# A hybrid encoder layer on one core: re-stacking of rotated heads through DRAM, tokens normalised ahead, and side tasks emitted by a model of when shared PSUM banks are read

## The chip, the cores and the metric

One core of one Trainium2 chip runs the whole layer as one program. The metric is the device time of one execution in microseconds (us); lower is better. Engines are named as in the profile: PE (TensorE, matrix products), PEld (its weight loads), DVE (VectorE), ACT (ScalarE), POOL (GpSimd), and SP (SyncE), whose queue issues every DMA of this kernel.

## What is computed

One encoder layer over 2048 tokens of width 1024 in float32. The normalised tokens are projected to about 4.6 thousand columns. Three groups of heads use them: windowed attention (16 query heads, 4 key/value heads, rotary, a sink logit), a state-space group that is scanned in both directions in chunks of 128 tokens, and 4 heads of attention into 256 memory tokens. The three are concatenated to 2048 columns, multiplied by `w_out`, added to the input and normalised.

```python
hn = rms_norm(h, norm_in_w); proj = hn @ w_in
q = rotary(q); k = rotary(k)
att = window_attention(q, k, v, sink) * silu(g_attn)
y = ssd_scan(xs, dt_f, ...) + ssd_scan(reversed ...) + d_skip * xs
ssd = gated_group_rmsnorm(y, z, ssd_norm_w)
xat = softmax(qm @ mk) @ mv * silu(g_mem)
h = h + concat(att, ssd, xat) @ w_out
out = rms_norm(h, norm_out_w)
```

## The kernel before, in words

Every large product is made of three: each operand is split into a high part (a cast on ACT) and a low part (a subtraction on DVE, `split`, L170 to L173), and high*high, high*low and low*high are accumulated in one PSUM bank (`split3`, all recorded at L154).

**Main line.** Tokens are taken in four windows `c` = 3, 2, 1, 0 of about 512 tokens. For each window the kernel projects keys (`keys`, L346), values and step sizes (`values`, L361), then for four head groups `g` the queries and gates (`heads`, L463), the convolution inputs, the gate `z` and one memory head. `prep_x` (L317) loads the next window's raw tokens, multiplies them by the norm and splits them into the 16 tiles `xh` and `xl`. After the last window comes the output projection: `out_block(c)` (L979) for the 16 blocks of 128 tokens. Each makes 96 products: 48 on the attention rows 0 to 3 and the memory rows 12 to 15 of `mix_d`, then 48 on its rows 8 to 11 (state-space part) and 4 to 7. One block (15) does its first 48 earlier, in `early` (L963), while attention is finishing.

**Side tasks.** Attention blocks, memory attention, the local part of the scan (`ssd_local`, L581), the incoming states (`incoming`, L696) and the gated norm of the scan (`forward`, L725) are Python generators. PE's order is exactly the order in which the program emits its products; the other engines' order is chosen by the scheduler. Each product adds an assumed time to `clock`. Between pieces of the main line `tick` (L112) resumes every side task whose `yield` time has passed on that clock; `need(task)` (L131) lets the clock run, with nothing emitted by the main line, until a task is done. A task counts as done when its last instruction is emitted.

**The scan's end.** `forward(c)` starts when `forward(c-1)` is done, and the first when `ssd_local` of the last window is done. It loads `y_d` into `b0`, adds the incoming states, multiplies by `z`, squares, yields 15; a small product with `ones` sums the squares (`t<-ones`); yields 4; a second small product spreads the scale (`t<-yo`); DVE then scales `b0` in four instructions (L758) and SP stores it to rows 8 to 11 of `mix_d` (L760). `out_block(c)` calls `need(fwd[c])` before its second 48 products and loads these rows back as `mxl` (L947); ACT makes `mxh` of them, DVE the low part.

**PSUM.** `pj` has three banks for the main line; `s` and `t` have two and `o` one, shared by all side tasks. A product into a bank waits until the bank's last reader is done.

**Re-stacking.** `rope` (L207) rotates two projected tiles with four products on DVE and two sums on POOL. `heads` then copies 32-partition pieces into the tile `qs` with 16 small DMAs (L475), and `keys` stores 16 pieces to `k_d` (L358). `values` has one buffer `gm` for what it stores to `v_d` (L375), one DMA for each block.

Of the kernel before, what the change touches and what calls it, by code (L numbers as in the profile page):

```python
# [17 lines left out]
P = 128  # L18
# [27 lines left out]
def layer(ctx: ExitStack, tc: tile.TileContext, a: dict):  # L46
# [22 lines left out]
    k_d = dram.tile([2, NG, 64, L], F32, name="k_d")  # L69
# [13 lines left out]

    def bank(pl, name):
        return pl.tile([P, 512], F32, name=name)

# [120 lines left out]
    def rope(pa, pb, cs, sn):  # L207
        n = cs.shape[-1]
        t1, t2, t3 = (misc.tile([P, CH], F32, name=f"rt{i}")[:, :n] for i in range(3))
        nc.vector.tensor_tensor(t1, pa, cs, ALU.mult)  # L210
        nc.vector.tensor_tensor(t3, pa, sn, ALU.mult)
        nc.vector.tensor_tensor(t2, pb, sn, ALU.mult)
        nc.gpsimd.tensor_tensor(t1, t1, t2, ALU.subtract)  # L213
        nc.vector.tensor_tensor(t2, pb, cs, ALU.mult)
        nc.gpsimd.tensor_tensor(t3, t3, t2, ALU.add)
        res = []
        for i, t in enumerate((t1, t3)):
            hi = as32r(misc.tile([P, CH], F32, name=f"r{'ht'[i]}{i}")[:, :n])
            split(hi, as32r(t), t)
            res.append((hi, as32r(t)))  # L220
        return res
# [95 lines left out]
    def prep_x(c, rb, raw=None):  # L317
        s, _ = window(c)
        w = CH * (c + 1) - s
        hs, ls = [], []  # L320
        for kt in range(KT):
            if raw is None:
                x32 = (misc.tile([P, XW + 6], F32, name="raw", bufs=2) if kt == 3 else
                       misc.tile([P, XW], F32, name="th", bufs=2) if kt in (4, 5) else
                       misc.tile([P, XW], F32, name="cu", bufs=3))[:, :w]
                nc.sync.dma_start(x32, a["xT"][kt * P:(kt + 1) * P, s:s + w])
                src = x32
            else:
                src = raw[kt]
                x32 = misc.tile([P, XW], F32, name="cu", bufs=3)  # L330
            nc.vector.scalar_tensor_tensor(x32, src, nw[:, kt:kt + 1], rb[:, :w], ALU.mult, ALU.mult)
            xh = xhl.tile([P, XW], F32R, name="xh")
            xl = xhl.tile([P, XW], F32R, name="xl")
            split(xh[:, :w], xl[:, :w], x32)
            hs.append(xh)
            ls.append(xl)
        return hs, ls

    def tables(t0, n):
        tab = misc.tile([P, 2, CH], F32, name="tab")[:, :, :n]  # L340
        nc.sync.dma_start(tab, a["trig"][:, :, t0:t0 + n])
        return tab[:, 0], tab[:, 1]
# [3 lines left out]
    def keys(c, xs):  # L346
# [4 lines left out]
        for o, pa in zip(range(0, e - s, n), pas):  # L351
            tab = tables(s + o, n)
            pb = yield from proj(wb, xs, o, n)
            res = rope(pa, pb, *tab)
            for j in range(2):
                for w in range(2):
                    for g in range(NG):
                        nc.sync.dma_start(k_d[w, g, j * 32:(j + 1) * 32, s + o:s + o + n],  # L358
                                          as32(res[j][w])[g * 32:(g + 1) * 32])

    def values(c, xs):  # L361
# [6 lines left out]
        for b in range(nb):  # L368
# [4 lines left out]
            v = misc.tile([P, CH], F32, name="gm")[:, :256]  # L373
            nc.scalar.mul(v, ps[:, :256], 0.5)
            nc.sync.dma_start(v_d[s // P + b], v)  # L375
# [3 lines left out]
    def steps(s, nb, raw):  # L379
# [21 lines left out]
        yield 8.0  # L401
# [6 lines left out]
        mm(pf[:, 256:256 + n], ones, raw.rearrange("p b r -> p (b r)"), True, True)  # L408
        fl = fc.rearrange("p b d r -> p (b d r)")
# [6 lines left out]
        yield 1.5  # L416
        pt = bank(ps_t, "t")
        nc.tensor.transpose(pt[:n, :P], fl, ident)
# [44 lines left out]
    def heads(c, xs, g, tab):  # L463
# [5 lines left out]
        res = rope(pa, pb, *tab)  # L469
        qs = ap_.tile([P, 4, CH], F32R, name="qs", bufs=2)  # L470
        for w in range(2):
            for j in range(2):
                for r in range(4):
                    o = w * 64 + j * 32
                    nc.sync.dma_start(as32(qs)[o:o + 32, r, :], as32(res[j][w])[r * 32:(r + 1) * 32])  # L475
# [7 lines left out]
    def attention(c, g, i, qs, gt, kv):  # L483
# [7 lines left out]
        if i == 4 * c:  # L491
            yield from take("kst", 1)
            kst = [ap_.tile([P, 6 * P], F32R, name=nm, bufs=2) for nm in ("khh", "kll")]
            for j in range(2):
                for u in range(2):
                    nc.sync.dma_start(as32(kst[j])[u * 64:(u + 1) * 64, :(hi + 1 - lo) * P],
                                      k_d[j, g, :, lo * P:(hi + 1) * P])
# [12 lines left out]
        for r in range(4):  # L510
            ss = bank(ps_s, "s")
            mm(ss[:, :w], qs[:, r, tl], kst[0][:, ks], True, False)
            mm(ss[:, :w], qs[:, r, tl], kst[1][:, ks], False, True)
            nc.vector.tensor_tensor_reduce(pm[:, r, :w], ss[:, :w], band[:, ms], 1.0,  # L514
                                           sink8[:, 4 * g + r:4 * g + r + 1], ALU.add, ALU.max, mx[:, r:r + 1])
            if r < 3:
                yield 1.2
# [13 lines left out]
        for n_, j in enumerate(order):  # L531
            if n_ == 2:
                yield 0.7
            tt = bank(ps_t, "t")
            for r in range(4):
                tr(tt[:, r * P:(r + 1) * P], pm[:, r, j * P:(j + 1) * P])
            if n_ == 1:
# [4 lines left out]
        held["pm"] += 4  # L542
        oo = bank(ps_o, "o")
        for j in order:
            vv = vg[:, k0 + j - lo]
            mm(oo[0:64, 0:256], vv, pts[j][:, 0:256], j == order[0], j == order[-1])
            mm(oo[64:128, 0:256], vv, pts[j][:, 256:512], j == order[0], j == order[-1])
        held["pt"] += nk
# [32 lines left out]
    def ssd_local(blocks):  # L581
# [3 lines left out]
        yield 5.0  # L585
        for i, (c, g) in enumerate(parts):
# [4 lines left out]
            xc, ee = nxt  # L591
            tt = bank(ps_t, "t")
            for j in range(3):
                tr(tt[:, j * P:(j + 1) * P], xc[:, j])
            nat = sp.tile([P, 3 * P], F32, name="nat", bufs=1)
            nc.scalar.copy(nat, tt[:, :3 * P])
            pc = bank(ps_s, "s")
            mm(pc[:, :P], xc[:, 2], xc[:, 3], True, True)
            cbm = sp.tile([P, 2, P], F32, name="cbm")
# [14 lines left out]
            yield 14.0  # L614
            py = bank(ps_o, "o")
            for pr in range(2):
                for u in range(2):
                    r = 2 * pr + u
                    mm(py[u * 64:(u + 1) * 64, pr * P:(pr + 1) * P], nat[:, r * 64:(r + 1) * 64], gg[:, r], True, True)
            yo = sp.tile([P, 2, P], F32, name="yo")  # L620
# [3 lines left out]
            nc.sync.dma_start(y_d[2 * g:2 * g + 2, :, c * P:(c + 1) * P].rearrange("j p t -> p j t"), yo)  # L624
            pst = bank(ps_s, "s")
            mm(pst, nat[:, 256:384], xd.rearrange("p d r e -> p (d r e)"), True, True)
            so = sp.tile([P, 2, 256], F32, name="carry")
# [22 lines left out]
    def mem_attention(c, hd, qh, ql, gm, mkt):  # L650
        yield 11.0
        pms = []
        for half in range(2):
            ss = bank(ps_s, "s")
            for j in range(2):
                tl = slice((2 * half + j) * P, (2 * half + j + 1) * P)
                for _ in split3(ss[:, j * MEM:(j + 1) * MEM], [(qh[:, tl], ql[:, tl], mkt[:, :MEM], mkt[:, MEM:])]):
                    pass
            mx = misc.tile([P, 2], F32, name="mmx", bufs=3)
# [16 lines left out]
        pts = []  # L676
        for m in range(2):
            tt = bank(ps_t, "t")
            for q in range(4):
                tr(tt[:, q * P:(q + 1) * P], pms[q // 2][:, q % 2, m * P:(m + 1) * P])  # L680
            hi = ap_.tile([P, 512], F32R, name="pt", bufs=3)
# [6 lines left out]
        yield 2.0  # L688
        oo = bank(ps_o, "o")
        for _ in split3(oo, [(mvt[:, 0, m], mvt[:, 1, m], pts[m][1], pts[m][2]) for m in range(2)]):  # L690
            pass
        held["pt"] += 2
# [3 lines left out]
    def incoming(c):  # L696
# [13 lines left out]
        yield 5.0  # L710
        for d, st_ in enumerate((state["f"], hbt)):
            py = bank(ps_s, "s")
            for pr in range(4):
                mm(py[:, pr * P:(pr + 1) * P], st_[:, pr * P:(pr + 1) * P], cc[:, pr // 2], True, True)
            nc.vector.tensor_tensor(ef[:, d], py.rearrange("p (q t) -> p q t", q=4), ef[:, d], ALU.mult)
            if d == 0:
                yield 1.0
# [7 lines left out]
    def forward(c):  # L725
# [18 lines left out]
        yield 15.0  # L744
        pn = bank(ps_t, "t")
        for g in range(2):
            mm(pn[:, g:g + 1], zv[:, g, 0], ones[:, 0:1], True, True)
# [343 lines left out]
```

## Time and profile before

| what | value |
|---|---|
| median of 3 runs | 1913.85 us (1912.57 to 1914.81) |
| the profiled execution | 1912.68 us |
| its span, first to last instruction | 1911.0 us |
| PE busy | 1780.5 us, 93% of the span |
| mean granted clock of TensorE | 0.973 of full speed |
| DMA queue | 305 MB, 52.9% of 16 engines' span |

The span is one execution as the profiler recorded it; the 1.7 us between it and that execution's time lie before the first and after the last instruction. Idle time of an engine is put down to what ended it. PE's share is the one near the span; the next is DVE with 62%.

### The profile page before, as it was taken

The page shows a single profiled execution, that of the slowest core. Times are in us where ns is not written, and L with a number is a line of the kernel's source. Part 1 is how long each engine was busy: PE and PEld are TensorE (multiplying, and loading weights), DVE is VectorE, ACT ScalarE, POOL GpSimd, SP SyncE. Part 2 cuts the span into 40 slices and gives each one's busy share as a digit, 9 for nine tenths or more (in the row PEclk, how much of TensorE's full clock was granted, in tenths as well). Part 3 has the DMA queues.
Part 4 walks back from the last instruction along what each step waited for, and adds up shares of the span by engine and source line. Part 5 has one row for each costly group of instructions (what it writes and reads, how often), then busy time and mean ns, then how long its engine had stood idle before and what let it go on. Part 6 is the DMA issues. An engine that isn't in the chain of part 4 may idle for free.

```text
span 1911.0 us, 27061 instructions
## 1 busy us (share of the span) xinstructions
PE 1780.5 (93%) x9242; PEld 1440.4 (75%) x9242; DVE 1187.4 (62%) x2709; ACT 928.7 (49%) x2006; POOL 331.5 (17%) x295
## 2 busy tenths in 40 slices
PE   6879999978999997999999989999898899999998
PEld 5767888856778785776778768776676688887886
DVE  6456566686776568677566778866775744333332
ACT  5247556563756555556456565456555521111111
POOL 0100000022220001222000012211222233323210
PEclk9989999999999999999999989999899999999999
DMA  6555343458654344756443457645456665555531
GB/s 226 155 149 168 117 131 112 121 167 251 204 170 138 103 133 138 220 181 189 135 136 111 131 179 234 194 134 176 146 181 192 201 196 166 166 164 171 160 122 55
DMA packets 254554, 306.75 MB, mean 161 GB/s; under 512 B 32848, under 2 KB 174928, under 8 KB 254416
## 3 DMA queue, kind: packets, MB, share of 16 engines
q1 hardware_dynamic: 254416, 305.02, 52.9%
q8 instruction: 73, 1.20, 0.3%
q14 instruction: 65, 0.53, 0.1%
HBM read 224.46 MB, written 63.70 MB: 151 GB/s over the span
## 4 chain that ended last, share of the span: by engine, by line
PE 59%; DVE 13%; DMA 13%; ACT 6%; issue 5%; SPq 2%; POOL 1%; DVEq 0%; ACTq 0%; POOLq 0%
PE pj L154 44%; PE s L154 7%; PE o L154 4%; PE t L158 3%; DVE wl L173 2%; DMA ws<-in_w_in_dram 2%; ACT pm L522 2%; DMA cu<-in_x_dram 2%; ACT wh L172 1%; DVE b L605 1%; ACT pm L526 1%; DVE pm L514 1%; DMA mxl<-mix_d 1%; DMA v_d<-gm 1%; PE t L154 1%
## 5 line engine op out<-in xcount | busy, mean ns | idle before, releaser
L154 PE MATMUL pj<-xh,wh 128*128 128x512 f32 (+2 forms) x1296 | 508.8, 393 | 9.2 <-ACT xh L172 6.5
L154 PE MATMUL pj<-xl,wh 128*128 128x512 f32 (+2 forms) x1296 | 498.0, 384 | 11.3 <-DVE xl L173 11.2
L154 PE MATMUL pj<-xh,wl 128*128 128x512 f32 (+2 forms) x1296 | 496.3, 383 | 0.8 <-DVE wl L173 0.7
L173 DVE TENSOR_TENSOR wl<-ws,wh 128x1024 fp32r<-128x1024 f32 (+2 forms) x175 | 219.1, 1253 | 117.9 <-ACT wh L172 111.8
L154 PEld LDWEIGHTS pj<-xl,wh 128*128 128x128 f32 x1296 | 248.0, 191 | 50.9 <-DVE xl L173 16.6
L154 PEld LDWEIGHTS pj<-xh,wh 128*128 128x128 f32 x1296 | 248.3, 192 | 49.2 <-ACT xh L172 7.6
L154 PEld LDWEIGHTS pj<-xh,wl 128*128 128x128 f32 x1296 | 247.5, 191 | 46.2 <-DVE wl L173 1.6
L172 ACT CAST wh<-ws 128x1024 fp32r<-128x1024 f32 (+2 forms) x175 | 179.9, 1028 | 153.6 <-PE pj L154 103.5
L522 ACT ACTIVATE pm<-pm,mx 128x385 f32<-128x385 f32 (+1 forms) x256 | 151.4, 594 | 78.1 <-DVE mx L520 78.0
L514 DVE CUSTOM_DVE_ANT_0 pm<-s,band,sink 128x384 f32<-128x384 f32 (+1 forms) x256 | 149.5, 595 | 58.9 <-PE s L154 56.6
L154 PE MATMUL pj<-woh,mxh 128*128 128x512 f32 x416 | 169.1, 406 | 1.9 <-ACT woh L172 1.9
L154 PE MATMUL pj<-wol,mxh 128*128 128x512 f32 x416 | 164.6, 396 | 2.0 <-DVE wol L173 2.0
L154 PE MATMUL pj<-woh,mxl 128*128 128x512 f32 x416 | 164.4, 395 | 0.0
L526 ACT ACTIVATE pm<-pm,den 128x384 f32<-128x384 f32 (+1 forms) x256 | 133.1, 592 | 17.4 <-DVE den L524 17.4
L172 ACT CAST mxh<-mxl 128x512 fp32r<-128x512 f32 x64 | 39.3, 618 | 184.8 <-DMA mxl<-mix_d 99.4
L154 PE MATMUL s<-khh,qs 128*128 128x384 f32 (+1 forms) x256 | 96.3, 376 | 20.7 <-DMA qs<-rt 8.9
L158 PE MATMUL t<-ident,pm 128*128 128x128 f32 x736 | 105.6, 279 | 9.7 <-ACT pt L540 3.8
L540 ACT COPY pt<-t 128x512 f32<-128x512 f32 x120 | 69.9, 582 | 90.2 <-PE t L158 90.0
L158 PEld LDWEIGHTS t<-ident,pm 128*128 128x128 f32 x736 | 88.2, 143 | 31.4 <-issue 6.0
L213 POOL TENSOR_TENSOR rt<-rt,rt 128x512 f32<-128x512 f32 (+2 forms) x21 | 28.5, 1358 | 470.4 <-DVE den L524 202.6
L451 DVE SCALAR_TENSOR_TENSOR cu<-raw,cw,cu 128x512 f32<-128x512 f32 (+2 forms) x128 | 98.3, 775 | 15.0 <-ACT cu L449 14.4
L173 DVE TENSOR_TENSOR mxl<-mxl,mxh 128x512 fp32r<-128x512 f32 x64 | 48.7, 760 | 90.8 <-ACT mxh L172 90.8
(228 smaller groups left out, 3001.5 us busy)
## 6 DMA issues: line engine op xcount, KB each, us to landing
ws<-in_w_in_dram SPq DMA_DIRECT2D x152, 512.0 KB, 4.0
fb<-f_d SPq DMA_DIRECT2D x32, 512.0 KB, 4.9
mxl<-mix_d SPq DMA_DIRECT2D x64, 256.0 KB, 4.0
qs<-rt SPq DMA_DIRECT2D x192, 64.0 KB, 2.1
mix_d<-ao SPq DMA_DIRECT2D x64, 128.0 KB, 3.1
xc<-xbc_d SPq DMA_DIRECT2D x32, 256.0 KB, 4.0
st_d<-carry SPq DMA_DIRECT2D x32, 256.0 KB, 3.6
fb<-ef_d SPq DMA_DIRECT2D x32, 256.0 KB, 4.2
```

The lines of the kernel that those rows point to most:

```text
L154: nc.tensor.matmul(out, lhsT=lhsT, rhs=rhs, start=start, stop=stop)
L158: nc.tensor.transpose(out, in_, ident)
L172: nc.scalar.copy(hi, x)
L173: (eng or nc.vector).tensor_tensor(lo, x, as32(hi), ALU.subtract)
L213: nc.gpsimd.tensor_tensor(t1, t1, t2, ALU.subtract)
L451: nc.vector.scalar_tensor_tensor(u, raw[:, r0 + k:r0 + k + cnt], cw[:, i, k:k + 1], u, ALU.mult, ALU.add)
L514: nc.vector.tensor_tensor_reduce(pm[:, r, :w], ss[:, :w], band[:, ms], 1.0, sink8[:, 4 * g + r:4 * g + r + 1], ALU.add, ALU.max, mx[:, r:r ...
L522: nc.scalar.activation(pm[:, r, :w + 1], pm[:, r, :w + 1], AF.Exp, bias=mx[:, r:r + 1], scale=0.125, accum_out=den[:, r:r + 1])
L526: nc.scalar.activation(pm[:, r, :w], pm[:, r, :w], AF.Copy, scale=den[:, r:r + 1])
L540: nc.scalar.copy(pts[j], tt)
L605: nc.vector.tensor_scalar(gg[:, r], cbm[:, 0], dt[:, 0, hd], None, ALU.mult)
```

## The change

It makes five edits. (1) `rope` works on both halves in one tile with instructions of 1024 columns, all on DVE and ACT; `heads` stores the high and the low half to `q_d` in DRAM and loads each back in stacked form (4 DMAs for 16); `keys` stores 2 for 16; the table has three rows. (2) `norm_x`, called after `heads` of group 2, loads the next window's tokens, normalises them and stores them to `xn_d`; `prep_x` loads them from there and only splits. (3) `values` stores two blocks in one DMA from a tile with three buffers. (4) `bank` notes on `clock` until when each bank of `s`, `t` and `o` will be read; before each use a task yields until the bank is taken to be free (`slot`), and `reads` sets that time. Fixed yields change with it, among them 8 to 18 and 1.5 to 2 in `steps`, 5 to 12 in `ssd_local`, 5 to 7 in `incoming`, 4 to 5.5 in `forward`. (5) The first early block takes its weights one after the other for both halves of the columns.

```diff
+    turn = {"s": 0, "t": 0, "o": 0}
+    until = {"s": [0.0] * 2, "t": [0.0] * 2, "o": [0.0]}
     def bank(pl, name):
+        if name in turn:
+            until[name][turn[name] % len(until[name])] = clock[0] + 3.0
+            turn[name] += 1
         return pl.tile([P, 512], F32, name=name)
+    def slot(name, n=1):
+        while True:
+            u = until[name]
+            t = max(u[(turn[name] + i) % len(u)] for i in range(n))
+            if t <= clock[0]:
+                return
+            yield max(t - clock[0], 0.1)
+    def reads(name, us, back=1):
+        u = until[name]
+        u[(turn[name] - back) % len(u)] = clock[0] + us
...
+    def rope(pa, pb, tab):
+        n = tab.shape[-1]
+        t, u = (misc.tile([P, 2, CH], F32, name=f"rt{i}")[:, :, :n] for i in range(2))
+        nc.vector.tensor_tensor(t, pa.unsqueeze(1).broadcast_to([P, 2, n]), tab[:, 1:3], ALU.mult)
+        nc.vector.tensor_tensor(u, pb.unsqueeze(1).broadcast_to([P, 2, n]), tab[:, 0:2], ALU.mult)
+        nc.vector.tensor_tensor(t, t, u, ALU.add)
+        hi = as32r(misc.tile([P, 2, CH], F32, name="rt1")[:, :, :n])
+        split(hi, as32r(t), t)
+        return hi, as32r(t)
...
+    def norm_x(c, rb):
+        s, _ = window(c)
+        w = CH * (c + 1) - s
+        for kt in range(KT):
+            x32 = misc.tile([P, XW], F32, name="xp", bufs=4)[:, :w]
+            nc.sync.dma_start(x32, a["xT"][kt * P:(kt + 1) * P, s:s + w])
+            nc.vector.scalar_tensor_tensor(x32, x32, nw[:, kt:kt + 1], rb[:, :w], ALU.mult, ALU.mult)
+            nc.sync.dma_start(xn_d[kt, :, s:s + w], x32)
...
-        yield 8.0
+        yield 18.0
+        yield from slot("t")
         pf = bank(ps_t, "t")
...
-                    nc.sync.dma_start(as32(qs)[o:o + 32, r, :], as32(res[j][w])[r * 32:(r + 1) * 32])
+        for w, t in enumerate(rope(pa, pb, tab)):
+            nc.sync.dma_start(q_d[g % 2][w], as32(t))
+            nc.sync.dma_start(as32(qs)[w * 64:(w + 1) * 64], q_d[g % 2][w].rearrange("(r p) j t -> (p j) r t", r=4))
...
+            yield from slot("s")
             ss = bank(ps_s, "s")
             mm(ss[:, :w], qs[:, r, tl], kst[0][:, ks], True, False)
             mm(ss[:, :w], qs[:, r, tl], kst[1][:, ks], False, True)
+            reads("s", 1.7)
...
         nxt = ssd_load(*parts[0])
-        yield 5.0
+        yield 12.0
...
-        yield 4.0
+        yield 5.5
+        yield from slot("t")
         pn = bank(ps_t, "t")
         mm(pn[:, :2 * P], ones, dg.rearrange("p g t -> p (g t)"), True, True)
+        reads("t", 2.0)
```

How the order moves, at three places. First, PE in the output projection, at the fifth block (`c` = 4). `t<-yo` is the small product of `forward(4)`; `woh8` to `woh11` are the weights for rows 8 to 11 of `mix_d`; `mxh` and `mxl` with a number are the two halves of one loaded piece. Before, `forward(4)`'s product stands among the second products of block 2:

```order
L154 MATMUL pj_15389<-wol9_14960,mxh_15470 128x512
L154 MATMUL pj_15389<-woh9_14961,mxl_15468 128x512
L154 MATMUL t_15518<-yo_15490,ones_107 128x256
L154 MATMUL pj_15389<-woh10_14967,mxh_15470 128x512
L154 MATMUL pj_15389<-wol10_14966,mxh_15470 128x512
```

and 170 rows later, the products of block 4 on its rows 8 to 11 begin with `mxh_15845`:

```order
L154 MATMUL pj_15761<-wol15_14774,mxh_15769 128x512
L154 MATMUL pj_15761<-woh15_14775,mxl_15767 128x512
L154 MATMUL pj_15760<-woh8_14781,mxh_15845 128x512
L154 MATMUL pj_15760<-wol8_14780,mxh_15845 128x512
L154 MATMUL pj_15760<-woh8_14781,mxl_15843 128x512
```

In the changed kernel the same block reads, with no row between the two:

```order
L177 MATMUL pj_15327<-wol15_14334,mxh_15335 128x512
L177 MATMUL pj_15327<-woh15_14335,mxl_15333 128x512
L177 MATMUL t_15397<-yo_15364,ones_110 128x256
L177 MATMUL pj_15326<-woh8_14341,mxh_15414 128x512
L177 MATMUL pj_15326<-wol8_14340,mxh_15414 128x512
L177 MATMUL pj_15326<-woh8_14341,mxl_15412 128x512
```

All 16 blocks of the changed kernel read like this: 16 `t<-yo`, each followed directly by the first product on `woh8` of its own block. For blocks 0 and 15 `t<-ones` also stands directly before `t<-yo`.

Second, SP at the same block of the changed kernel: `b0_15221` is what `forward(4)` scaled, `mxl_15412` the piece that the products above need.

```order
L1037 DMA xr_15521<-in_x_dram 128x1024
L807 DMA mix_d_102<-b0_15221 128x4x128
L776 DMA b0_15404<-y_d_93 128x4x128
L993 DMA mxl_15412<-mix_d_102 128x4x128
L993 DMA mxl_15417<-mix_d_102 128x4x128
L993 DMA mxl_15511<-mix_d_102 128x4x128
```

Before, the store of `forward(4)` and the load of the same rows stand ten issues apart on SP; now only the next block's `y_d` load is between them.

Third, PE where attention ends and the scan's end begins. Before, the first products of `incoming` (`s<-cbm,state`) stand among the last attention blocks:

```order
L154 MATMUL s<-mkt,qh 128x256 x2
L154 MATMUL s<-mkt,ql 128x256
L154 MATMUL s<-cbm,state 128x128 x4
L154 MATMUL s<-khh,qs 128x384
L154 MATMUL s<-kll,qs 128x384
```

Now `ssd_local` is emitted up to row 5497 of PE's order, and they follow at row 5532, 84 rows later than before (row 5448), inside the early block's products:

```order
L181 MATMUL t<-ident,pm 128x128 x4
L177 MATMUL s<-cbm,state 128x128 x4
L177 MATMUL pj<-woh_14335,mxh 128x512
L177 MATMUL pj<-wol_14334,mxh 128x512
L177 MATMUL pj<-woh_14335,mxl 128x512
L177 MATMUL s<-cbm,b_14422 128x128 x4
```

In the first window, the step-size product `t<-dtraw` stands 42 projection products later than before (row 462 for row 420).

## Rows read from the trace of the kernel before

**Rows 1.** The page: busy time, share of the span and instructions of each engine.

```profile
PE 1780.5 (93%) x9242; PEld 1440.4 (75%) x9242; DVE 1187.4 (62%) x2709; ACT 928.7 (49%) x2006; POOL 331.5 (17%) x295
```

**Rows 2.** Stages: each engine's busy time and count, granted clock, DMA share, GB/s.

```profile
412.00:1462.00 1050.00, 990.74 (x5208) 785.97 (x5207) 736.04 (x1774) 601.51 (x1327) 174.87 (x153) 0.97 0.55 165
1462.00:1510.00 48.00, 32.29 (x177) 24.70 (x178) 35.61 (x76) 31.94 (x75) 20.24 (x14) 0.93 0.67 206
1510.00:1903.80 393.80, 391.17 (x1840) 320.64 (x1837) 154.22 (x307) 74.49 (x144) 100.53 (x93) 1.00 0.53 155
```

**Rows 3.** What PE waited for: us in total, times, longest.

```profile
PE pj L154 <- DVE xl L173: 11.2, 11, 1.6
PE t L154 <- DVE dtraw L400: 10.4, 1, 10.4
PE s L154 <- DVE mx L514: 9.3, 11, 2.1
...
PE s L154 <- DMA qs<-rt: 8.9, 3, 5.1
PE s L154 <- ACT mpm L665: 8.5, 6, 2.3
PE pj L154 <- ACT xh L172: 6.5, 2, 4.4
...
PE pj L154 <- ACT dtraw L376: 5.4, 2, 4.9
PE t L158 <- ACT pt L540: 4.0, 5, 1.4
...
PE o L154 <- DVE ao L550: 3.8, 3, 1.3
```

**Rows 4.** Three stretches, columns as in rows 2, each just after a wait of PE.

```profile
76.60:80.00 3.40, 3.39 (x15) 3.40 (x16) 1.40 (x4) 0.72 (x2) 2.00 (x2) 0.50 0.20 62
...
110.50:114.10 3.60, 3.60 (x12) 3.12 (x13) 1.09 (x3) 0.51 (x2) 1.04 (x1) 0.50 0.45 109
...
473.30:479.40 6.10, 6.10 (x17) 5.33 (x18) 3.48 (x10) 0.00 (x0) 0.00 (x0) 0.50 0.81 267
```

**Rows 5.** Chain of waits, 1684 to 1731: start, us, what.

```profile
1687.38 0.63 ACT mxh L172
...
1688.64 1.13 DVE b L758 x4
...
1689.78 2.27 DMA mix_d<-b
...
1707.65 0.08 DVE rn L749
...
1709.16 0.67 PE t L154 x2
```

**Rows 6.** DMA issues: line, queue, times, KB each, median us from issue to landing.

```profile
mxl<-mix_d SPq DMA_DIRECT2D x64, 256.0 KB, 4.0
...
mix_d<-b SPq DMA_DIRECT2D x16, 256.0 KB, 2.4
...
v_d<-gm SPq DMA_DIRECT2D x16, 128.0 KB, 4.7
```

**Rows 7.** Tile `mxl`, from 1530: min/median/max ns of each; us from issue to landing.

```profile
L173 DVE TENSOR_TENSOR mxl<-mxl,mxh x56: 677/692/1553, 1537.6 to 1879.2; 128x512 fp32r<-128x512 f32 x56
L947 SPq DMA_DIRECT2D mxl<-mix_d x55: 359/384/954, 1536.6 to 1870.4; - x55
...
DMA to landing us min/median/max: 2.5/4.0/5.7
```

**Rows 8.** Chain of waits, whole span: the last products after the last `t<-yo`.

```profile
1852.25 51.61 PE pj L154 x222
```

**Rows 9.** Tile `rt` (rotated heads): min/median/max ns of SP's copies to `qs`.

```profile
L475 SPq DMA_DIRECT2D qs<-rt x192: 507/588/1582, 108.8 to 1427.7; - x192
```

More of the change, by code (lines that the diff above doesn't have):

```diff
@@ L66, in layer @@
     misc = pool("misc", 1, stack=wx)
-    k_d = dram.tile([2, NG, 64, L], F32, name="k_d")
+    k_d = dram.tile([2, P, 2, L], F32, name="k_d")
+    q_d = [dram.tile([2, P, 2, CH], F32, name=f"q_d{i}") for i in range(2)]
+    xn_d = dram.tile([KT, P, L], F32, name="xn_d")
     xbc_d = dram.tile([8, P, L], F32, name="xbc_d")
@@ L339, in tables @@
     def tables(t0, n):
-        tab = misc.tile([P, 2, CH], F32, name="tab")[:, :, :n]
+        tab = misc.tile([P, 3, CH], F32, name="tab")[:, :, :n]
         nc.sync.dma_start(tab, a["trig"][:, :, t0:t0 + n])
-        return tab[:, 0], tab[:, 1]
+        return tab
     dts = {}
@@ L353, in keys @@
             pb = yield from proj(wb, xs, o, n)
[L354 to L359, printed above, removed]
+            for w, t in enumerate(rope(pa, pb, tab)):
+                nc.sync.dma_start(k_d[w, :, :, s + o:s + o + n], as32(t))
     def values(c, xs):
@@ L372, in values @@
                                  wv[k // 3][1][:, (k % 3) * NV:(k % 3 + 1) * NV]) for k in range(KT)])
-            v = misc.tile([P, CH], F32, name="gm")[:, :256]
-            nc.scalar.mul(v, ps[:, :256], 0.5)
-            nc.sync.dma_start(v_d[s // P + b], v)
+            if b % 2 == 0:
+                m = min(2, nb - b)
+                v = misc.tile([P, XW], F32, name="cu", bufs=3)[:, :m * 256].rearrange("p (m d) -> p m d", m=m)
+            nc.scalar.mul(v[:, b % 2], ps[:, :256], 0.5)
+            if b % 2 == m - 1:
+                nc.sync.dma_start(v_d[s // P + b - m + 1:s // P + b + 1].rearrange("b p d -> p b d"), v)
             nc.scalar.copy(raw[:, b, :], ps[:, 256:NV])
@@ L516, in attention @@
             if r < 3:
-                yield 1.2
+                yield 0.6
         if i == 4 * c + 3:
@@ L531, in attention @@
         for n_, j in enumerate(order):
-            if n_ == 2:
-                yield 0.7
+            yield from slot("t")
             tt = bank(ps_t, "t")
@@ L542, in attention @@
         held["pm"] += 4
+        yield from slot("o")
         oo = bank(ps_o, "o")
@@ L591, in ssd_local @@
             xc, ee = nxt
+            yield from slot("t")
             tt = bank(ps_t, "t")
@@ L614, in ssd_local @@
             yield 14.0
+            yield from slot("o")
             py = bank(ps_o, "o")
@@ L653, in mem_attention @@
         for half in range(2):
+            yield from slot("s")
             ss = bank(ps_s, "s")
@@ L676, in mem_attention @@
         pts = []
+        yield from slot("t", 2)
         for m in range(2):
@@ L687, in mem_attention @@
             pts[m] = tt, hi, lo
-        yield 2.0
+        yield 3.0
+        yield from slot("o")
         oo = bank(ps_o, "o")
@@ L691, in mem_attention @@
             pass
+        reads("o", 1.4)
         held["pt"] += 2
@@ L709, in incoming @@
             nc.sync.dma_start(ef[u * 64:(u + 1) * 64], ev[u].partition_broadcast(64))
-        yield 5.0
+        yield 7.0
         for d, st_ in enumerate((state["f"], hbt)):
+            yield from slot("s")
             py = bank(ps_s, "s")
@@ L744, in forward @@
         yield 15.0
+        yield from slot("t")
         pn = bank(ps_t, "t")
@@ L911, in layer @@
             with tc.high_priority(offset=200):
-                xs = prep_x(c - 1, rb)
-            idle(clock[0] + 0)
+                xs = prep_x(c - 1)
     need(mem_t)
@@ L968, in early @@
         nc.sync.dma_start(xr, a["x"][c * P:(c + 1) * P, :])
-        for n_ in products(pf, mh, ml, [(n_, k) for n_ in range(2) for k in mh], WO_K[0], WO_K[7]):
+        order = [(n_, k) for k in mh for n_ in range(2)]
+        if begun:
+            order.sort(key=lambda v: v[0])
+        for n_ in products(pf, mh, ml, order, WO_K[0], WO_K[7]):
             if n_ is not None:
```

63 lines of the change are left out of this document (27 added, 36 removed).

## The prediction

> **What bounds the kernel now.** I read the busy shares first: PE is busy for 1780.5 of 1911.0 us, the next engine, DVE, for 62% [rows 1]. So time is lost or won where PE stands still or runs at the lower clock. The stages say where that is: between 412 and 1462 PE lacks 59 of 1050 us, in the 48 us at the end of attention 16, but in the output projection from 1510 to 1903.8 only 2.6 of 393.8, at a clock of 1.00 [rows 2]. That stage has nothing to give and can only lose. The waits name the causes ahead of it, none over 11.2 us in total [rows 3]. A wait also costs clock: after waits of 4.9, 10.4 and 5.1 us [rows 3] PE was busy at a granted clock of 0.50, its lower level of 1.2 GHz, for 3.4, 3.6 and 6.1 us [rows 4].
>
> **The change, part by part.**
>
> *The scan's end against the output projection.* This decides. `forward` yields longer and starts later (`ssd_local` yields 12 for 5), so `out_block(c)` now meets `need(fwd[c])` unfulfilled. The emitting loop lets its own clock run until `t<-yo` is emitted, takes the task as done, and emits the 48 products that use its result. The order shows it for all 16 blocks. Before, 170 rows lay between for block 4, and 222 products of 51.61 us follow the last `t<-yo` [rows 8], 0.2325 us each; the way from `t<-yo` to the product was hidden under them. Now no row of PE hides it:
>
> - DVE scales `b0`, four instructions: 1.13 us [rows 5].
> - SP stores it: 2.27 us to landing [rows 5], median 2.4 [rows 6].
> - SP issues `b0<-y_d`, which overwrites the stored tile and so waits for that landing: 0.36 to 0.38 us, as its like [rows 7].
> - `mxl` lands 4.0 us after its issue [rows 6].
> - ACT makes `mxh`: 0.63 us [rows 5].
> - About 0.3 us of hops between them, estimated from the gaps of some hundredths of a us in that chain.
>
> That is 8.7 us. The third product needs the low part, 0.69 us of DVE [rows 7] against two products of 0.23, so 0.3 more: 9.0 us of idle PE for each block. Behind the waiting product stand all others, since PE takes them in this order. Then the lower clock: half of 3.4, 3.6 and 6.1 us [rows 4] is 1.7, 1.8 and 3.05 us, mean 2.2. So 11.2 us a block, 16 blocks: **179 us**. With the shortest landing of `mxl`, 2.5 us, and 1.7 of clock it is 9.4 us a block, with the longest, 5.7, and 3.05 it is 13.8 [rows 4, 7]: 150 to 220 us. I take the medians, as nothing in the new order crowds the queue more than before. For blocks 0 and 15 `t<-ones` and `t<-yo` are neighbours too: from `rn` at 1707.65 to `t<-yo` at 1709.16 is 1.5 us [rows 5], twice **3 us**.
>
> The Trainium skill (DMA: Bandwidth & Descriptors, section Anatomy of one DMA) gives about 2.0 us fixed plus the bytes at 436 GB/s, by which my estimate for 256 KB is 2.6 us. The store's rows, 2.27 and 2.4, agree; the load's median of 4.0 does not. By the Trainium skill's formula the store and the load would cost 5.2 us instead of 6.3 and the sum would be some 18 us lower.
>
> *Step sizes.* `t<-dtraw` stood 10.4 us [rows 3] and cost 1.8 of clock behind it [rows 4]. It now stands 42 products later, 9.6 us at 0.2275 to 0.2325 each, so I take all of it: **-12.2**. The cover is weights for these products; if they are late the gain goes to them.
>
> *Values.* `gm` was one buffer, and its store took 4.7 us to land [rows 6]; ACT held the `pj` banks meanwhile: 5.4 us [rows 3] and 1.7 of clock [rows 4]. Three buffers and half the stores end that: **-7.1**.
>
> *Shared banks.* Waits for the readers `mx`, `mpm`, `pt` and `ao` are 9.3 + 8.5 + 4.0 + 3.8 = 25.6 us [rows 3]. The model puts a product of the main line between where there is one; at the end of attention there is little, and its times of 1.3 to 3.0 us are guesses. Between 0 and 25.6 I take half: **-13**.
>
> *Re-stacking.* PE waited 8.9 us for `qs` [rows 3]. SP spent 16 issues of 588 ns [rows 9], 9.4 us, for each group; now four, but the chain is a store, its landing and a load, on rows of 2.4 and 4.0 [rows 6] or more, since the pieces are 512 KB. What is queued on SP behind a load that waits for a landing are weights. Between -8.9 and +10 I take **-3**.
>
> *Tokens ahead.* PE waited 17.7 us for `xh` and `xl` [rows 3], mostly at the three window changes. The norm leaves that path, the split and four of eight loads stay on it, since `xp` has four buffers. 24 stores and 24 loads of 320 KB come on top, on SP too. Between -17.7 and +20 I take **-3**.
>
> *At nothing:* `rope` on DVE, eight 512-column passes for six, under DVE's 38% idle time; POOL loses its two sums at 17% busy; 10 `k_d` stores for 80; the third table row; the order in the early block; the smaller DMA scratch. If PE stopped waiting on other things, `rope` would show in the `pj` banks.
>
> **Sum.** 1912.7 (the profiled execution) + 179.2 + 3 - 12.2 - 7.1 - 13 - 3 - 3 = 2056.6. The median of the runs is 1.2 us above that execution: **2058 us**, slower.
>
> **The rivals.**
>
> *Short landings.* While PE stands, fewer transfers are under way, so `mxl` lands in its shortest 2.5 us [rows 7]: 16 times 1.5 less, 2034. For it: the store lands faster in a quiet queue. Against: `y_d` and three more pieces are issued around it. Chance 0.18. The Trainium skill's formula above gives nearly this time.
>
> *The model of the banks does nothing.* `clock` is not the chip's time, and the 13 us stay: 2071. For it: the banks are read when DVE and ACT come to it, and the waits for `mx`, up to 2.1 us each [rows 3], are longer than the 1.7 us that the model allows. Chance 0.20.
>
> *Another queue becomes the bound.* In the windows SP stands behind landings: 24 reloads of tokens and 32 of `qs`. If half of these 56 hold the weights for 3 us each as far as PE, 84 us come on top: 2142. For it: two weight buffers only, 5.6 us of products each. Against: SP saves 12 issues of 0.59 us per group [rows 9] and no wait for weights is among the large ones [rows 3]. Chance 0.09.
>
> *The other side: PE runs on past the waiting product.* 24 products on rows 4 to 7 of the same block, 5.6 us, and 48 of the next block, 11.2, do not need the scan. If PE took them first, the 9.0 us would be covered, and only the gains stay: 1912.7 - 38.3 + 1.2 = 1876, faster. It decides where less than 38.3 / 16 = 2.4 us a block stays uncovered. Against it: at `t<-dtraw` PE stood for 10.4 us [rows 3] with products behind it that needed nothing more. Chance 0.05.
>
> **How the numbers follow.** The forecast itself keeps 0.48. Ends of the two large unknowns, 150 to 220 for the blocks and -11 to 72 for the gains, give 1995 to 2148 if all fall together; two in ten left out, with 2142 and 1876 among them, leaves **2010 to 2112**. A measurement of this kernel tells about 0.2%, 3.8 us, from no change. Faster 0.05, same 0.01, slower 0.94.
>
> **What would show it.** In the output projection of the changed kernel PE should stand 16 times for 8 to 10 us, released by ACT `mxh` or DVE `mxl`, some 11 us further apart than their products take; the stage should be 150 us or more longer and its granted clock below 1.00; the chain should run DVE `b`, `mix_d<-b`, `mxl<-mix_d`, ACT `mxh` in every block. The waits for `dtraw` L400 and L376 should be gone, those for `mx` and `mpm` about halved. If the output stage keeps its 394 us, the whole argument is wrong; if it grows but the stages ahead of it do too, the third rival is right.

## The result and the profile after

The changed kernel takes 2055.43 us (median of 4 runs, 2049.35 to 2061.84) against 1914.33 us (median of 4 runs of the kernel before): a ratio of 1.0734, 95% interval 1.0695 to 1.0772. It is slower by 141 us; the forecast was 2058. The profiled execution shown here took 2061.84 us with a span of 2060.1.

Read first the busy times on the page of the changed kernel (engine, busy us, share of the span, instructions), then the granted clock in 40 slices of the span, in tenths:

```profile
PE 1803.4 (88%) x9242; PEld 1457.6 (71%) x9242; DVE 1183.7 (57%) x2667; ACT 920.7 (45%) x1985; POOL 265.9 (13%) x253
...
PEclk9999999999999999999999999999988989888897
```

Beside [rows 1], PE has the same 9242 products but 88% of a longer span, and its busy time itself grew by 23 us. The last quarter of the clock row says why: it is below 9 in most slices. That quarter is the output projection. Stretches of the changed kernel: two cut as in [rows 2], the stage from its first product on `w_out`, and two short ones around waits (columns: stretch, length, then busy us and count for PE, PEld, DVE, ACT, POOL, then granted clock, DMA share, GB/s):

```profile
412.00:1462.00 1050.00, 974.59 (x5156) 775.16 (x5156) 735.22 (x1764) 602.67 (x1333) 127.80 (x122) 0.97 0.61 184
1462.00:1510.00 48.00, 37.24 (x200) 28.19 (x198) 31.67 (x44) 23.24 (x36) 16.49 (x10) 0.94 0.74 238
1471.00:2053.00 582.00, 440.84 (x1912) 352.93 (x1910) 172.21 (x330) 81.33 (x156) 122.60 (x108) 0.87 0.40 119
1688.90:1695.70 6.80, 2.90 (x7) 2.28 (x8) 2.13 (x4) 2.56 (x5) 2.95 (x2) 0.50 0.85 235
1900.50:1914.20 13.70, 7.31 (x16) 5.29 (x17) 4.14 (x5) 3.00 (x5) 2.54 (x2) 0.50 0.59 153
```

and the same stage of the kernel before, from its first product on `w_out`:

```profile
1495.00:1903.80 408.80, 401.65 (x1889) 328.80 (x1889) 168.27 (x320) 86.38 (x165) 109.48 (x98) 1.00 0.54 160
```

The stage went from 408.8 to 582.0 us, so 173.2 us more. Idle PE is the length less the busy time: 7.2 before, 141.2 now, so 134.0 more. The other 39.2 us are PE's busy time: the clock at 0.87 in place of 1.00, and 23 more products that now fall behind the cut (1912 for 1889). Everything ahead of the stage is 24 us shorter (1495 to 1471). The sum, 149.2, is the difference of the two profiled executions (2061.84 less 1912.68).

What PE waited for in the changed kernel (engine, tile and line, releaser: us in total, times, longest):

```profile
PE pj L177 <- ACT mxh L195: 127.3, 16, 8.5
PE s L177 <- DMA qs<-q_d: 41.3, 10, 10.6
PE s L177 <- DVE mx L539: 9.2, 12, 1.7
PE pj L177 <- ACT memh L829: 9.0, 1, 9.0
PE t L177 <- DVE yo L798: 7.9, 1, 7.9
PE t L181 <- ACT nat L625: 7.4, 1, 7.4
PE o L177 <- ACT pt L565: 7.2, 2, 4.5
PE t L181 <- ACT pt L565: 6.9, 6, 2.3
...
PE pj L177 <- DVE rt L235: 5.5, 1, 5.5
...
PE pj L177 <- DVE xl L196: 2.9, 2, 1.6
...
PE o L177 <- DVE mpm L725: 2.2, 5, 1.0
PE o L177 <- DVE ao L577: 0.6, 1, 0.6
```

Sixteen waits for `mxh`, one for each block of 128 tokens, make up nearly all of the 134.0 us. Beside [rows 3], the waits for `dtraw` and `xh` are gone, `xl` and `mpm` are small, `mx` has not moved, and the wait for `qs` is nearly five times as long. One block of the chain of waits in the changed kernel (start, us, what):

```profile
1684.96 1.13 DVE b L805 x4
...
1686.12 2.31 DMA mix_d<-b
...
1688.44 0.37 SPq L776
...
1688.86 3.19 DMA mxl<-mix_d
...
1692.13 0.63 ACT mxh L195
...
1692.80 11.35 PE pj L177 x42
```

From the end of `t<-yo` at 1684.94 to the first product at 1692.80 it is 7.86 us, through four instructions of DVE, a store, an issue, a load and a cast, with PE standing. Behind it 42 products take 11.35 us; at the 0.2325 us each of [rows 8] they would take 9.8. The granted clock was 0.50, the level of 1.2 GHz, from 1688.9 to 1695.7, as the stage rows show; around another of these waits it lasted from 1900.5 to 1914.2. In all there are 16 such stretches in this stage, 6.8 to 17.1 us long, and PE was busy for 77.8 of their 157.0 us (the sum over the 16):

```profile
sum 157.02, PE 77.78; mean PE 4.86
```

The Trainium skill (TensorE: Matmul & The Clock Gate, Part 1) says that the clock depends on how busy PE has been of late; these rows agree, with their 0.50 around each of the 16 waits.

### The profile page after: what moved, and what is told of

The parts are those of the page before. It is cut to its first block, busy times and chain, and to the rows that moved or that the text cites. A ratio compares the mean times of both kernels' runs of the same rounds, so it can differ in the third digit from the quotient of the medians.

```text
span 2060.1 us, 26491 instructions
## 1 busy us (share of the span) xinstructions
PE 1803.4 (88%) x9242; PEld 1457.6 (71%) x9242; DVE 1183.7 (57%) x2667; ACT 920.7 (45%) x1985; POOL 265.9 (13%) x253
## 4 chain that ended last, share of the span: by engine, by line
PE 62%; DMA 17%; DVE 10%; ACT 5%; issue 4%; POOL 1%; SPq 1%; DVEq 0%; POOLq 0%; ACTq 0%
PE pj L177 46%; PE s L177 7%; PE o L177 4%; DMA qs<-q_d 4%; PE t L181 4%; DMA mxl<-mix_d 3%; DMA q_d<-rt 2%; DMA mix_d<-b 2%; DVE wl L196 2%; DMA ws<-in_w_in_dram 1%; DMA cu<-in_x_dram 1%; ACT wh L195 1%; DVE b L805 1%; ACT pm L547 1%; DMA xp<-in_xT_dram 1%
## 5 line engine op out<-in xcount | busy, mean ns | idle before, releaser
L177 PE MATMUL pj<-woh,mxh 128*128 128x512 f32 x416 | 184.0, 442 | 127.3 <-ACT mxh L195 127.3
L196 DVE TENSOR_TENSOR wl<-ws,wh 128x1024 fp32r<-128x1024 f32 (+2 forms) x175 | 213.5, 1222 | 89.6 <-ACT wh L195 78.2
L177 PEld LDWEIGHTS pj<-woh,mxh 128*128 128x128 f32 x416 | 87.2, 210 | 151.6 <-ACT mxh L195 134.0
L177 PE MATMUL pj<-woh,mxl 128*128 128x512 f32 x416 | 176.8, 425 | 2.9 <-DVE mxl L196 2.9
L177 PE MATMUL pj<-wol,mxh 128*128 128x512 f32 x416 | 177.2, 426 | 0.0
L177 PE MATMUL s<-khh,qs 128*128 128x384 f32 (+1 forms) x256 | 96.8, 378 | 49.4 <-DMA qs<-q_d 41.3
L641 POOL TENSOR_TENSOR b<-nat,win 128x256 f32<-128x256 f32 x64 | 42.3, 680 | 679.9 <-ACT nat L625 665.6
```

Of the source, the lines that this page charges most:

```text
L177: nc.tensor.matmul(out, lhsT=lhsT, rhs=rhs, start=start, stop=stop)
L196: (eng or nc.vector).tensor_tensor(lo, x, as32(hi), ALU.subtract)
L641: nc.gpsimd.tensor_tensor(xd[:, d], nat[:, 0:256].rearrange("p (r e) -> p r e", r=4), win[:, d, 4 * g:4 * g + 4].unsqueeze(2).broadcast_to ...
```

## Experiments

The theory on trial: the cost is the way from `t<-yo` to `mxh`, uncovered because the order leaves no row of PE between the scan's end and the product that needs it. I call the rows between them the lead. Counted in PE's order it was 125 to 225 rows in the kernel before; now the needing product is the very next row, a lead of 1, in all 16 blocks. The rivals: the changed transfers make the stage slow, or the waits would come back elsewhere. Each kernel was compared with the kernel before, run beside it.

**The lead given back.** `e1_lead_both` takes the changed kernel and puts back two pauses; the leads become 97 to 237 rows.

```diff
# ssd_local
-        yield 12.0
+        yield 5.0
# forward
-        yield 5.5
+        yield 4.0
```

> The changed kernel with two yields as before: the first of ssd_local 12 to 5, the last of forward 5.5 to 4. Everything else of the change stays. In the order 158 to 237 rows of PE (97 at least) now lie between each block's scaling product and the product that uses it. Theory (missing cover in the output projection, which grew from 408 to 582 us): all 16 waits for mxh go, the stage returns to some 410 us, time 1883 us (2055 less 172). Rival (the DRAM round trips and the bank model cost it, the order of the scan's end is a side effect): 2020 us or more.

Measured: 1868.07 us, ratio to the kernel before 0.9783 (0.9757 to 0.981). No wait for `mxh` is left; the stage from the first product on `w_out` is 408.1 us long, with 3.4 idle. Its row, columns as in the stage rows above:

```profile
1456.00:1864.50 408.50, 405.08 (x1925) 332.23 (x1923) 178.78 (x342) 86.14 (x166) 114.92 (x103) 1.00 0.57 169
```

Two numbers turn a loss of 141 us into a gain of 44, and all else of the five edits stays in place. The time is 15 us below the expected 1883, since the part ahead of the stage is shorter too (first product on `w_out` at 1456 for 1471).

`e2_lead_start` puts back only the first pause: the lead is 151 to 157 rows for 13 blocks and 107, 55 and 1 for the last three. `e3_lead_grows` puts back only the second: the lead is 1 at the first block and grows by some 6 rows with each (1, 7, 13, 19, 25, 31, 37, 44 and so on).

> The changed kernel with the first yield of ssd_local alone back from 12 to 5: the lead is 151 to 157 rows for blocks 0 to 12, 107, 55, and 1 row for block 15. Theory: one wait of 7.9 us with its clock is left, 1883 + 11 = 1894 us. Rival that forward's longer yield sets its pace and so costs by itself: every block stays as long as in the changed kernel, 2040 us or more.

> The changed kernel with the last yield of forward alone back from 5.5 to 4: the lead starts at 1 row and grows by 6 a block: 1, 7, 13, 19, 25, 31, 37 and so on. Theory, by dose: each row covers 0.2325 us of the 7.9, so the waits are 7.9, 6.5, 5.1, 3.7, 2.3, 0.9 and none, 26 us and some 8 of clock: 1917 us. Rival (a fixed cost a block, whatever the lead): 2055 us; rival (only a full lead of 150 rows helps, since the loads crowd): over 1960 us.

Measured: 1884.78 us (0.9861, 0.9837 to 0.9885) with one wait of 7.5 us, at the last block, and 1939.97 us (1.015, 1.0124 to 1.0177). The waits of the second kernel:

```profile
PE s L177 <- DMA qs<-q_d: 36.3, 8, 9.8
PE pj L177 <- ACT mxh L195: 31.3, 7, 7.6
```

The seven, in order of time, are 7.61, 6.48, 5.64, 3.87, 3.61, 2.41 and 1.70 us: each block that has more rows of cover waits less, and from the eighth block none waits. That is the direction that the theory asks for, but the step is 0.99 us on average and not the 1.4 us that 6 more rows of 0.2325 us take [rows 8]. The way to be covered grew with the lead: the store of the scaled rows landed in 2.28 to 2.29 us in the first three blocks and in 2.69, 3.71 and 4.05 in the next three, and the load of the seventh took 4.66. The time missed its expectation by 23 us, although the base of 1883 was 15 too high. In the profiled executions the output stage is 53 us longer than in `e1_lead_both`, where 34 were expected, with one wait of 5.8 for `yo` among it, and the part ahead of it is 12 us longer, where nothing was.

**The lead taken from the kernel before.** `e4_before_late` has of the five edits only the last pause of `forward`, and a further pause that starts the scan later:

```diff
+            yield 30.0   # forward, once, ahead of the first block
-        yield 4.0
+        yield 5.5
```

> The kernel before, with two numbers changed and nothing else of the change: forward(0) yields 30 more before it begins, and forward's last yield is 5.5 for 4. The order then has 1 row between in all 16 blocks, as in the changed kernel. Theory: the cost appears without any of the five edits: 16 waits of some 8 us and 2 to 2.4 of clock each, 1914 + 165 = 2080 us, with some more for the late start. Rival (the DRAM round trips and the bank model are needed for it): 1914 to 1930 us.

Measured: 2067.43 us, ratio 1.0812 (1.0777 to 1.0848). Its waits:

```profile
PE pj L154 <- ACT mxh L172: 128.3, 16, 10.1
PE s L154 <- DMA qs<-rt: 11.9, 3, 6.2
```

The same 16 waits with the same total. So this loss needs neither the DRAM round trip nor the bank model: only the lead. The rest of the change is not without a part, though. By the ratios, losing the lead costs 182 us in the changed kernel (0.9783 to 1.0734) and 155 in the kernel before (1 to 1.0812); put the other way, all else of the five edits is worth 41 us with the lead kept and 15 without. Where the 27 us between them come from was not tried.

**The re-stacking.** `e5_restack_direct` is `e1_lead_both` with the round trip undone: 8 copies of 64 KB from `rt` to `qs` where a store and a load stood.

```diff
-            nc.sync.dma_start(q_d[g % 2][w], as32(t))
-            nc.sync.dma_start(as32(qs)[w * 64:(w + 1) * 64], q_d[g % 2][w].rearrange(...))
+            for j in range(2):
+                for r in range(4):
+                    nc.sync.dma_start(as32(qs)[w * 64 + j:(w + 1) * 64:2, r, :], as32(t)[r * 32:(r + 1) * 32, j, :])
```

> The kernel of e1_lead_both (1868.1 us) with the queries re-stacked as in the kernel before, chip memory to chip memory, in 16 DMAs of 64 KB for each 4 of the round trip. Theory (the serial round trip through DRAM is what made the wait for qs grow from 8.9 to 32.7 us): the wait falls to 8 to 12 us, and the time to 1868 - 22 = 1846 us, some us lower if clock comes back too. Rival (SP's queue was the price): each piece issues 16 DMAs of about 0.59 us in place of 4 of 0.33 and 0.61 us, some 7.5 us more on SP, 120 us over 16 pieces; weights issued behind them come late, the wait moves to products waiting for w or to mx, and the time stays at 1865 to 1885 us.

Measured: 1838.83 us, ratio 0.9631 (0.9601 to 0.9662), 29 us better than `e1_lead_both` and the fastest kernel of this study. PE's wait for `qs` in it:

```profile
PE s L177 <- DMA qs<-rt: 9.4, 4, 6.3
```

The chains show the exchange. In `e1_lead_both`, in the second window:

```profile
449.31 1.06 ACT rt L195
...
455.66 8.30 DMA qs<-q_d
...
464.06 1.62 PE s L177 x4
```

and in `e5_restack_direct`, where SP's issues themselves stand in the chain:

```profile
446.68 1.06 ACT rt L195
...
455.38 0.59 SPq L499
456.02 2.12 DMA qs<-rt
458.23 0.94 PE s L177 x4
```

From the end of the cast to the first score product it is 13.7 us through DRAM (450.37 to 464.06) and 10.5 directly (447.74 to 458.23). The load in the first chain is a long one, 8.30 us for a median of 6.0. SP does pay for 8 issues of 0.59 us, but each small copy lands fast and they overlap; the two 512 KB transfers come one after the other. Rows of the DMA issues of `e1_lead_both` (line, queue, times, KB each, median us to landing):

```profile
q_d<-rt SPq DMA_DIRECT2D x32, 512.0 KB, 4.7
qs<-q_d SPq DMA_DIRECT2D x32, 512.0 KB, 6.0
```

and of `e5_restack_direct`:

```profile
qs<-rt SPq DMA_DIRECT2D x256, 64.0 KB, 2.9
```

`e12_direct_alone` makes the same edit in the changed kernel itself, with its lead of 1 row.

> The changed kernel (2055.4 us) with the re-stacking alone undone; the lead stays at 1 row for all 16 blocks. Theory (the terms add, since they lie in different stages): the 16 waits for mxh stay at 7.5 to 8.5 us each, qs falls from 41.3 to about 10 us, and the time is 2055 - 29 = 2026 us, by the 29 us that e5_restack_direct gained on e1_lead_both. Rival (SP's queue or the scan's end take the gain back while the lead is gone): 2045 to 2060 us.

Measured: 2033.78 us (2023.2 to 2039.59), ratio 1.0639 (1.0607 to 1.0672), 22 us better than the changed kernel's 2055.43, or 18 by the ratios. The 16 waits stayed at 123.5 us in all; `qs` fell to 24.6, not 10. It lies between the two expectations: the terms lie in different stages and nearly add, as far as runs that are 16 us apart among themselves can tell.

**Tokens ahead.** `e6_tokens_at_change` is `e1_lead_both` with the loads and the norm back in `prep_x`, without `norm_x` and `xn_d`; the four buffers `xp` of the change stay.

```diff
-                nc.sync.dma_start(x32, xn_d[kt, :, s:s + w])
+                nc.sync.dma_start(x32, a["xT"][kt * P:(kt + 1) * P, s:s + w])
+                nc.vector.scalar_tensor_tensor(x32, x32, nw[:, kt:kt + 1], rb[:, :w], ALU.mult, ALU.mult)
```

> The kernel of e1_lead_both (1868.1 us) with the tokens loaded and normalised at the change of window, as in the kernel before. Theory (normalising ahead removed the waits for xh and xl, 17.7 us before against 2.9 in e1_lead_both): xh and xl come back as waits of 12 to 18 us and the time is 1880 to 1886 us. Rival (the extra write and read of the tokens only fill other waits): the waits come back but others fall by as much, 1866 to 1872 us.

Measured: 1874.62 us (1863.73 to 1876.42), ratio 0.9804 (0.9762 to 0.9845), which overlaps that of `e1_lead_both`. The waits for the tokens did not come back:

```profile
PE pj L177 <- DVE xl L196: 2.8, 2, 1.6
```

So the 14.8 us that are gone of the 17.7 of [rows 3] were not saved by normalising ahead. What else differs at this place from the kernel before is that the tokens now have buffers of their own, where they shared `raw`, `th` and `cu` with other steps, and that the emission around `prep_x` moved; which of these it is was not tried.

**Bank model.** `e7_no_bank_model` is `e1_lead_both` with `slot` returning at once; `e9_fixed_pauses` also puts back three fixed pauses that the model had replaced.

```diff
# e7, e9: slot
-            if t <= clock[0]:
-                return
+            return
# e9: scores, third transpose, incoming
-                yield 0.6
+                yield 1.2
-            yield from slot("t")
+            if n_ == 2:
+                yield 0.7
-                yield 0.6
+                yield 1.0
```

> The kernel of e1_lead_both (1868.1 us) with slot returning at once: the bank model holds nothing back, the other edits stay. The forecast's term for the shared banks was -13 us: by that the waits for mx, mpm, ao and pt come back (25.6 us before; 15.7 mx, 3.3 mpm and 7.4 pt in e1_lead_both) and the time is 1878 to 1886 us. Rival (the model does nothing for the time by itself): 1863 to 1872 us, with the same kinds of waits. The lead of the output projection stays large (127 to 223 rows), so no waits for mxh by either.

> The kernel of e7_no_bank_model (1922.6 us: the bank model off) with the fixed pauses of the kernel before put back where the model had replaced them: 1.2 between two score products, 0.7 ahead of the third transpose, 1.0 between the two directions of the incoming states. Theory (what the model itself is worth against fixed pauses is what e1_lead_both gains over this kernel; e7 lacked both): the waits for pt (32.6 us in e7) fall only in part, to 15 to 25, and the time is 1900 to 1915 us, so the model is worth 30 to 45 us. Rival (the pauses did the same work as the model, and e7 was slow because it had neither): pt back at about 7, time 1870 to 1885 us.

Measured: 1922.64 us (1.0069, 1.0046 to 1.0092) and 1889.06 us (0.9887, 0.9869 to 0.9906). Against `e1_lead_both` the model is worth 54.6 us where nothing else spaces the products, of which fixed pauses give 33.6; over them it is worth 21.0. Both forecasts for `e9` were missed: it lies between them. Waits of `e7_no_bank_model`:

```profile
PE t L180 <- ACT pt L564: 21.2, 40, 2.5
...
PE t L180 <- DVE pt L562: 11.4, 13, 1.7
```

The transposes into the two `t` banks wait 53 times for the reader of the bank. In `e9_fixed_pauses` the two rows come to 4.9 us, so the fixed pauses end most of these waits; which waits the model's further 21.0 us come from is not shown.

`e10_scores_later` and `e11_scores_longest` start from `e5_restack_direct` and raise the model's reading time of a score bank.

```diff
# e10 / e11
-            reads("s", 1.7)
+            reads("s", 2.0)   # e11: 2.4
# e11, ssd_local
-            yield 14.0
+            yield 12.0
```

> The kernel of e5_restack_direct (1838.8 us) with the model's reading time of a score bank at 2.0 in place of 1.7. The lead of the output projection falls to 73 to 168 rows, 17 to 39 us, still over 7.7. Theory (the model's time is shorter than the reader's, so PE still waits 15.9 us for mx): waits for mx fall by a third, to 10 to 12 us, and the time to 1833 us. Rival (the pause only shifts products that another wait then stops): 1837 to 1842 us.

> As e10_scores_later with a reading time of 2.4 us, and the pause of 14 ahead of the scan's output products at 12, which keeps the lead at 127 to 223 rows. Theory: waits for mx fall to 4 to 7 us, the time to 1828 to 1832 us, unless the shorter pause brings waits for the scan's gated factors (a few us). Rival: 1837 to 1845 us.

Measured: 1840.83 us (0.9638, 0.9618 to 0.9657), the same as `e5_restack_direct`, and 1873.82 us (0.982, 0.9798 to 0.9843), 35 us worse. The top waits of `e11_scores_longest`:

```profile
PE s L177 <- DMA qs<-rt: 24.0, 4, 10.3
PE t L181 <- DMA xc<-xbc_d: 9.6, 2, 5.6
...
PE s L177 <- DVE mx L540: 8.4, 9, 2.1
```

`mx` fell from 15.9 to 8.4 us as its theory said, but `qs` rose by 14.6, `xc` by 7.4, and `mpm` by 5.5 to 7.3: two changed pauses moved other products that hang on the same clock. Both theories missed this; which of the two pauses did it was not tried.

**Step sizes.** `e8_dt_soon` is `e1_lead_both` with the pause of 18 in `steps` back at 8.

> The kernel of e1_lead_both (1868.1 us) with the pause ahead of the decay's products at 8 as in the kernel before, not 18. Theory (the longer pause removed the wait of 10.4 us for dtraw at L400 of the kernel before, forecast as -12.2 us): a wait of about 10 us for dtraw comes back once and the time is 1876 to 1882 us. Rival (with the bank model ahead of those products the pause does not decide): no such wait, 1866 to 1870 us.

Measured: 1868.34 us (0.9781, 0.9743 to 0.9818), no wait for `dtraw`. The rival is right. In the first window of `e8_dt_soon` (engine, tile, count, duration, start):

```profile
L398 ACT COPY dtraw<-pj x5: 163/167/168, 70.3 to 89.5; 128x16 f32<-128x16 f32 x5
...
L422 DVE TENSOR_TENSOR dtraw<-dt,aneg x1: 242/242/242, 100.7 to 100.7; 128x80 f32<-128x80 f32 x1
```

and of the kernel before:

```profile
L376 ACT COPY dtraw<-pj x5: 162/167/168, 68.2 to 96.1; 128x16 f32<-128x16 f32 x5
...
L400 DVE TENSOR_TENSOR dtraw<-dt,aneg x1: 241/241/241, 110.1 to 110.1; 128x80 f32<-128x80 f32 x1
```

The last copy of raw step sizes is 6.6 us earlier, and the tile that PE needs is ready at 100.9 in place of 110.3. PE comes to it at 101.2. So the earlier end of `values` already removed the wait, and the later row in the order was not needed.

## Why the prediction was right, and which of its terms were not

**The deciding step held.** The forecast put 16 waits of 9.0 us and 2.2 us of clock behind each on the block's path, and 3 us for the two neighbours `t<-ones` and `t<-yo`: 182.2 in all. Measured are 173.2. One block waits 7.96 us (127.3 / 16), 1 less, mostly because `mxl` landed in 2.98 to 3.80 us, 3.24 on average, in the 15 blocks where the chain shows it, and not in the 4.0 of [rows 6]: the rival of short landings was half right. The clock cost 2.43 us a block (half of the 77.8 us for which PE was busy at 0.50, by 16), near the 2.2 taken from [rows 4]. The store's 2.27 us, the 1.13 of DVE and the 0.63 of ACT [rows 5] came back as 2.31, 1.13 and 0.63. The Trainium skill (DMA: Bandwidth & Descriptors, section Anatomy of one DMA) gives the formula, by which I estimated 2.6 us for 256 KB, for DMAs that GpSimd issues, and these are issued by SP. The estimate is under every one of the 15 loads, and the median of 4.0 is over every one. The range has a slip: with the shortest landing and 1.7 of clock a block comes to 9.2 us and 147 in all, not 9.4 and 150.

**Undersized:** block 0. `t<-yo` waited 7.9 us for `yo`, not 1.5. `t<-ones` had ended at 1499.75, but DVE came to `rn` only at 1504.20 and POOL to its step at 1505.37, both behind other work:

```profile
1504.20 0.15 DVE L794 TENSOR_SCALAR rn<-t 128x2 f32<-128x2 f32 x1
```

The forecast counted from the start of `rn` and put the way from `t<-ones` to it at nothing.

**The gains ahead of the stage** were forecast as 38.3 us and came to 24. The 24 are not the edits' alone: in `e4_before_late`, which has of them only one pause, the first product on `w_out` comes at 1476.3, 19.5 earlier than before, with 62 products fewer ahead of it (7291 for 7353). The parts of the forecast:

- *Step sizes* (-12.2): the wait of 10.4 us is gone as forecast, but not by the longer pause on which the term rested; `e8_dt_soon` shows it gone without.
- *Values* (-7.1): the wait at L376 is gone. A new one of 5.5 us, for `rt` at L235, stands where the keys are rotated. `rope` shows in the `pj` banks, as the forecast's line on what would be late next had it, but not by DVE's own time: its tile is still being stored to `k_d`, a store that the forecast put at nothing. The store ends at 72.46, and DVE begins at 72.58:

```profile
67.37 5.09 DMA k_d<-rt
```

- *Shared banks* (-13): the four waits went from 25.6 to 18.9 us (9.2, 2.2, 6.9 and 0.6), -6.7, and new ones for `nat` and `pt` of 7.4 and 7.2 came beside them, so by the waits nothing was won. By time the model does more than they tell: 21 us over fixed pauses, 54.6 over none, measured where the lead is kept. There the rival that it does nothing fell; in the changed kernel itself no run takes the model out.
- *Re-stacking* (-3): the sign was wrong. The wait grew from 8.9 to 41.3 us, and undoing it is worth 29 us in `e5_restack_direct`, 22 in `e12_direct_alone`; its upper bound of +10 was less than half of that. The step that failed is the middle value between a saving of issues and a serial chain: the chain was sized with rows of 256 KB, 2.4 and 4.0 us, where the pieces are 512 and take longer. The chain ahead of the longest wait for `qs` in the changed kernel (10.6 us, to 460.06) has

```profile
446.96 6.57 DMA q_d<-rt
...
453.54 6.38 DMA qs<-q_d
```

and that ahead of the longest in the kernel before (5.1 us, to 473.24) has SP's issues and one short landing:

```profile
470.39 0.59 SPq L475
...
471.03 2.17 DMA qs<-rt
```

- *Tokens ahead* (-3): `xh` and `xl` fell from 17.7 to 2.9 us, far better than forecast, but `e6_tokens_at_change` shows that the path through `xn_d` is not the cause.

So that the total was met within 3 us is luck: by the stages, a cost 9 us too large stood against gains 14 us too large, and the median of the runs lies 6.4 us below the profiled execution. By the runs, with and without the two pauses, the cost was 182 and the gains 41, both nearer to the forecast; but part of the 182 lies ahead of the stage, where the forecast had none, and the 41 hold a loss of 29 that it did not see and some 45 us of gain that no run assigns.

**The other rivals.** PE did not run on past the waiting product: 24 products of the same block need only rows 4 to 7, and PE stood in front of all. SP holding back weights did not show either; among PE's large waits none is for `w`, apart from 5.9 us for `wl`.

**What stays open.** From the kernel before to `e1_lead_both` it is 43.7 us. Undone one at a time, the bank model over fixed pauses gives 21.0, the path of the tokens 6.6 (within its interval of nothing), the longer pause none, and the re-stacking -29.2. That leaves some 45 us, if the terms add, for the parts not undone: the paired stores of values, `rope` in wide instructions, the keys' stores, the tokens' own buffers, the early block's order and the other pauses. The waits that are gone or smaller in `e1_lead_both` (14.8 of 17.7 for the tokens, all 15.8 for `dtraw`) point to the first and the fourth, which is argued and not shown.

## What to carry to other kernels

A planner that counts a task as done when its last instruction is emitted, and not when its result has landed, can place a consumer directly behind its producer; count the rows of the in-order engine between the two in the emitted order, price the way between them from the chain of the trace, and compare. A pause or reading time in such a planner acts on everything that shares its clock: here one reading time raised by 0.7 us and one pause lowered by 2 together cost 35 us, and two other pauses made the difference between 141 us lost and 44 won. And before small copies are merged into a round trip, set the two chains side by side from the data to the consumer, at the size that each transfer will have: here the issues and one short landing were less than a store and a load.

## What the runs showed of the hardware

- Eight copies of 64 KB within the chip's memory, issued 0.59 us apart, with a median landing of 2.9 us, delivered sooner than one store and one load of 512 KB with medians of 4.7 and 6.0 us. I had expected the number of issues to count for more.
- In the output projection of the changed kernel the granted clock was 0.50 in 16 stretches of 6.8 to 17.1 us, each beginning in or beside a wait of about 8 us. PE was busy for 2.9 to 7.3 us of each, 4.86 on average, so a wait cost 2.43 us of clock on top of its own length. [rows 4] show 3.4 to 6.1 us busy, about the same.
